# A fp32 network kernel: one 512-column product takes the place of two 256-column ones, and a preparation is spread over two stages

## The chip, the core and the metric

The kernel runs on one core of a Trainium2 chip. The metric is device time in microseconds (us) of one execution. Three runs of the kernel before gave 1077.32 us as the median (1076.91 to 1077.44).

## What is computed

Two layers on 256 tokens (S = 256) of width 1024 (D), in float32. Each layer is a SwiGLU of half weight, a mixer, a second SwiGLU of half weight and a gated embedding ("ple"), each behind an RMS norm. The mixer of layer 0 ("even") holds latent attention and gated linear attention, that of layer 1 ("odd") a gated linear recurrence (RG-LRU) and a complex diagonal state space (S5). What matters here:

```python
def rms_norm(x, g):
    y = x * lax.rsqrt(jnp.mean(x * x, axis=-1, keepdims=True) + EPS)
    return y * g

def swiglu(x, w1, w3, w2):          # D -> 2816 -> D
    return (jax.nn.silu(x @ w1) * (x @ w3)) @ w2

def even_mixer(xn, w_in, ...):
    c_q, c_kv, k_r, gq, gk, gv, g_low, g_r = split_cols(xn @ w_in, EVEN_IN_SPLITS)
    y_a = mla(c_q, c_kv, k_r, ...)
    y_b = gla(gq, gk, gv, g_low, g_r, ...)
    return jnp.concatenate([y_a, y_b], axis=-1) @ w_out

def odd_mixer(xn, w_in, ...):
    x_gate, x_rg, u = split_cols(xn @ w_in, ODD_IN_SPLITS)
    y_c = rg_lru_branch(x_gate, x_rg, ...)
    y_d = s5_branch(u, ...)         # a_re, a_im, log_dt, b, c: parameters only
    return jnp.concatenate([y_c, y_d], axis=-1) @ w_out
```

## The kernel before

**Layout.** Activations lie transposed: 128 channels on the partitions, 256 tokens in the free dimension, so the state h is eight tiles of 128x256. TensorE (PE) multiplies a 128x128 block of weights, which it holds, by a "moving" operand of 256 columns. Float32 accuracy comes from splitting both operands into a high part, a cast to the type fp32r, and a low part, the rest. A step of 128 inner channels (a **k-step**) is three products into the same half bank of PSUM (`mm3`, L260 to L266): high weights by high x (L264), high weights by low x (L265), low weights by high x (L266). Each product is preceded by a load of its weights (PEld).

**Weights** come once from memory. `fetch` (L230 on) issues a transfer of a 128x1024 chunk (SyncE, L242) into one of five raw buffers, ScalarE (ACT) casts the high part wh (L244), VectorE (DVE) subtracts to give the low part wl (L245); five pairs are in flight. A chunk serves one **group** of eight k-steps.

**Norms.** x = h times a gain is split at once (`feed`, ACT L307 and DVE L308); the squares are summed over channels (`stat` L312 on, L351), the reciprocal root R is made by a chain of small operations on GpSimd (POOL, L327 to L340), spread to all partitions by two PE transposes (L365) and a copy on ACT (L367). R is multiplied in only behind the first product, so PE starts a stage without it. `first4` (L272 on) runs the first four groups with the k-steps outermost, since x arrives tile by tile.

**Stages.** The order is ffn_a0, mix0, ffn_b0, ple0, ffn_a1, mix1, ffn_b1, ple1. In a SwiGLU (`ffn`, L377 on) **w1** is 44 groups (22 values of f, two groups each, 352 k-steps): the two groups of one f fill the halves of one PSUM bank, and the epilogue makes ab = bank times R (DVE, L388, 128x512), silu (ACT), s = their product (DVE, L393), and its split into gh (ACT, L289) and gl (DVE, L290). In **w2** (176 k-steps) each of eight output tiles m takes 22 k-steps over gh and gl, and h is updated by one DVE operation (L439). PSUM has five banks "mm" and three "aux". The first stage has its own hand-written start of three f, with squares on POOL.

**What sets the order.** In the mixers and at the start the order on PE is written by hand; everywhere else a scheduler orders each engine's queue when the kernel is built. A queue runs strictly in that order. The even mixer begins with `first4` and two more groups, whose six results are scaled by R into the latents cc (DVE L614, L627) and split after a gain (DVE L625), with squares added (L621); then PE goes to `linear_q`, two groups with the weights gq0 and gq1. The odd mixer begins with `first4` for the S5 input: four results times R, written in another order of tokens (us, DVE L1173), moved in blocks to other partitions (u4, copies on DVE L1178 and ACT), and multiplied into states (PE L1136), which a recurrence on DVE turns into XS (L1139 to L1155); outputs are PE L1163. ple0 scales its gate products by R (DVE, z, L470).

**S5 preparation** (`s5_prep`, L902 on) depends on parameters only: many operations of 128x16 and some of 128x256 on DVE. It is cut into steps, which `beside` puts between the groups of ffn_a1, two for every f up to 16 and three for every m from 1 on. Two of its results lie in x buffer A.

## Time and profile before

| | us |
|---|---|
| median of three runs | 1077.32 |
| span of the profiled execution, first to last instruction | 1074.8 |
| TensorE busy | 1047.1 |
| VectorE busy | 755.6 |
| ScalarE busy | 567.5 |
| GpSimd busy | 83.8 |

The span is 2.5 us shorter than the median; what lies outside of it is the launch. A matmul's start is measured, its end is modelled, and matmuls overlap in the rows, so the cost of one is read as the distance from its start to the next one's start, not as the duration in its row. A row with "x3" holds three instructions in one stretch. Where the clock of TensorE was at its lower level (1.2 GHz), "PEclk" in a table of stretches is 0.50; at 2.4 GHz it is 1.00.

### The profile page before, as it was taken

The numbers are of one execution on the slowest core, as the hardware profiler recorded it, in microseconds if no ns is written. First come the engines' busy times: TensorE is split into PE (matmuls) and PEld (weight loads), VectorE is DVE, ScalarE is ACT, GpSimd is POOL, SyncE is SP. The second block draws the span as 40 slices with busy tenths as digits, with TensorE's granted clock in tenths as the row PEclk, the third lists the DMA queues.
The fourth block names the chain that finished last, engine by engine and source line by source line (L and its number), as shares of the span: only waits on it lengthen the run. The fifth ranks groups of instructions, "written<-read, shape, count | busy, mean of one in ns | idle before, by whom it ended". The sixth has DMA issues, their size and how long they took to land.

```text
span 1074.8 us, 21027 instructions
## 1 busy us (share of the span) xinstructions
PE 1047.1 (97%) x8540; PEld 1025.4 (95%) x8540; DVE 755.6 (70%) x1298; ACT 567.5 (53%) x891; POOL 83.8 (8%) x180
## 2 busy tenths in 40 slices
PE   8899999989999999999999999999998999999996
PEld 7899999979799999999999999999897999999996
DVE  6766665487576766656589986877977766666664
ACT  5444444356465544445555664643778554444553
POOL 6200000230000000000151000002100000000000
PEclk8999999998999999999999999999999999999999
DMA  7655556554235655566626655555223555555651
GB/s 238 214 179 182 181 181 198 169 184 134 85 100 156 235 183 189 168 187 197 216 88 208 196 196 186 182 183 176 74 94 133 182 182 187 181 178 183 189 178 40
DMA packets 52690, 182.56 MB, mean 170 GB/s; under 512 B 5856, under 2 KB 6256, under 8 KB 52592
## 3 DMA queue, kind: packets, MB, share of 16 engines
q1 hardware_dynamic: 52592, 181.20, 52.1%
q8 instruction: 67, 1.10, 0.4%
q14 instruction: 31, 0.25, 0.1%
HBM read 180.13 MB, written 1.05 MB: 169 GB/s over the span
## 4 chain that ended last, share of the span: by engine, by line
PE 91%; DVE 3%; ACT 3%; POOL 2%; issue 1%; DMA 1%; SPq 0%; ACTq 0%; DVEq 0%; POOLq 0%
PE mm L264 27%; PE mm L266 27%; PE mm L265 27%; DVE wl L245 1%; PE aux L1121 1%; PE aux L1136 1%; ACT us L1166 1%; PE mm L501 1%; PE mm L503 1%; PE mm L502 1%; PE mm L715 1%; PE mm L717 1%; DMA h<-in_xT_dram 1%; PE mm L716 1%; PE mm L807 0%
## 5 line engine op out<-in xcount | busy, mean ns | idle before, releaser
L245 DVE TENSOR_TENSOR wl<-raw,wh 128x1024 fp32r<-128x1024 f32 (+2 forms) x350 | 420.9, 1207 | 159.1 <-ACT wh L244 158.1
L244 ACT CAST wh<-raw 128x1024 fp32r<-128x1024 f32 (+2 forms) x350 | 354.6, 1019 | 280.2 <-PE mm L265 128.6
L265 PE MATMUL mm<-xlA,wh 128*128 128x256 f32 x1200 | 341.8, 285 | 1.6 <-DVE xlA L308 1.6
L264 PE MATMUL mm<-xhA,wh 128*128 128x256 f32 x1200 | 341.4, 285 | 1.7 <-ACT xhA L307 1.7
L266 PE MATMUL mm<-xhA,wl 128*128 128x256 f32 x1200 | 340.6, 284 | 0.1
L265 PEld LDWEIGHTS mm<-xlA,wh 128*128 128x128 f32 x1200 | 231.2, 193 | 2.8 <-DVE xlA L308 2.7
L264 PEld LDWEIGHTS mm<-xhA,wh 128*128 128x128 f32 x1200 | 231.5, 193 | 1.9 <-ACT xhA L307 1.9
L266 PEld LDWEIGHTS mm<-xhA,wl 128*128 128x128 f32 x1200 | 231.5, 193 | 0.3 <-DVE wl L245 0.3
L264 PE MATMUL mm<-gh,wh 128*128 128x256 f32 x704 | 195.0, 277 | 0.0
L265 PE MATMUL mm<-gl,wh 128*128 128x256 f32 x704 | 194.9, 277 | 0.0
L266 PE MATMUL mm<-gh,wl 128*128 128x256 f32 x704 | 194.8, 277 | 0.0
L264 PE MATMUL mm<-xhB,wh 128*128 128x256 f32 x576 | 165.1, 287 | 2.5 <-DVE z L470 2.5
L266 PE MATMUL mm<-xhB,wl 128*128 128x256 f32 x576 | 164.1, 285 | 0.0
L265 PE MATMUL mm<-xlB,wh 128*128 128x256 f32 x576 | 164.1, 285 | 0.0
L266 PEld LDWEIGHTS mm<-gh,wl 128*128 128x128 f32 x704 | 132.2, 188 | 0.0
L264 PEld LDWEIGHTS mm<-gh,wh 128*128 128x128 f32 x704 | 132.2, 188 | 0.0
L265 PEld LDWEIGHTS mm<-gl,wh 128*128 128x128 f32 x704 | 132.0, 188 | 0.0
L264 PEld LDWEIGHTS mm<-xhB,wh 128*128 128x128 f32 x576 | 111.8, 194 | 2.7 <-issue 2.6
L265 PEld LDWEIGHTS mm<-xlB,wh 128*128 128x128 f32 x576 | 111.7, 194 | 0.0
L266 PEld LDWEIGHTS mm<-xhB,wl 128*128 128x128 f32 x576 | 111.6, 194 | 0.0
L289 ACT CAST gh<-s 128x256 fp32r<-128x256 f32 x88 | 35.5, 406 | 90.0 <-DVE s L393 90.0
L388 DVE TENSOR_TENSOR ab<-mm,R 128x512 f32<-128x512 f32 x82 | 56.4, 689 | 34.1 <-PE mm L266 31.9
(404 smaller groups left out, 1086.1 us busy)
## 6 DMA issues: line engine op xcount, KB each, us to landing
raw<-in_w_dram SPq DMA_DIRECT2D x308, 512.0 KB, 3.7
raw<-in_w_dram SPq DMA_DIRECT2D x36, 384.0 KB, 3.1
raw<-in_w_dram SPq DMA_DIRECT2D x6, 256.0 KB, 4.2
h<-in_xT_dram SPq DMA_DIRECT2D x4, 256.0 KB, 5.6
out_dram<-hg SPq DMA_DIRECT2D x4, 256.0 KB, 2.2
bd<-in_bd_dram SPq DMA_DIRECT2D x1, 512.0 KB, 4.6
gain<-in_fnorm_dram SPq DMA_DIRECT2D x1, 512.0 KB, 4.2
...
```

Source lines behind the costliest of these rows:

```text
L244: nc.scalar.copy(wh[:, sl], raw[:, sl])
L245: self.last_split = nc.vector.tensor_sub(wl[:, sl], raw[:, sl], wh[:, sl].bitcast(F32))
L264: mm(out, wh, xh, start=start, stop=False)
L265: mm(out, wh, xl, start=False, stop=False)
L266: mm(out, wl, xh, start=False, stop=stop)
L289: self.nc.scalar.copy(hi, src)
L388: nc.vector.tensor_mul(ab, src[0].rearrange("p (t s) -> p t s", t=2), R[:, None, :].to_broadcast([P, 2, S]))
L501: mm(pt, a, wh, start=k == 0, stop=False)
L502: mm(pt, b, wh, start=False, stop=False)
L503: mm(pt, a, wl, start=False, stop=k == KD - 1)
L715: mm(pg[name][i], a, wh, start=k == 0, stop=False)
L716: mm(pg[name][i], b, wh, start=False, stop=False)
```

## The change

**Products.** The tiles of x and of the SwiGLU's inner result become one tile each, in which the high and low part of a k-tile lie side by side ([P, KD, 2, S], [P, NF, 2, S]). `mm2` takes the place of `mm3` where these move past weights: one product of 512 columns (high weights by high and low part) into a whole bank of PSUM, and one of 256 columns (low weights by high part) into its lower half. A k-step is two products and two weight loads instead of three. The halves of the bank are added afterwards: `joined` copies the upper half to SBUF on ACT (128x256) and adds the lower on DVE (128x256); in w2 and in the mixers' output product, h is updated twice instead. `mm2` is used in all of w1 (1408 k-steps) and w2 (704), the input of the even mixer (48), the S5 input and the recurrence's two inputs in the odd mixer (96), both mixers' output products (128) and ple0's gate (64), 2448 k-steps in all. The linear attention's q and k, the latent up-projections, the token-major products and the last embedding keep three products. A SwiGLU's f takes two banks instead of one.

**Preparation.** `s5_prep` starts in ffn_b0 and stops at a mark behind the output matrices; the rest runs in ffn_a1, its input matrices last. `beside` is called once for every f and three times for every m. The tiles that the preparation keeps are allocated before ffn_b0 instead of before ffn_a1, so the SwiGLU's inner tile g lies at another address in ffn_b0 too.

In the built program PE has 5725 rows in its order instead of 8189 (repeats in one row), DVE 1485 instead of 1262, ACT 1021 instead of 820.

```diff
...
+    def mm2(self, out, w, c, x2, start, stop):
+
+        mm = self.nc.tensor.matmul
+        wh, wl = w[0][:, c : c + P], w[1][:, c : c + P]
+        both = x2.rearrange("p t s -> p (t s)")
+        if stop and not start:
+            mm(out[:, :S], wl, x2[:, 0, :], start=False, stop=False)
+            mm(out, wh, both, start=False, stop=True)
+        else:
+            mm(out, wh, both, start=start, stop=False)
+            mm(out[:, :S], wl, x2[:, 0, :], start=False, stop=stop)
+
+    def proj2(self, out, w, c0, x, nk):
+        for k in range(nk):
+            self.mm2(out, w, c0 + k * P, x[:, k], k == 0, k == nk - 1)
+
+    def joined(self, dst, pt):
+
+        self.nc.scalar.copy(dst, pt[:, S:])
+        self.nc.vector.tensor_add(dst, pt[:, :S], dst)
+        return dst
...
-        pts = [self.psum()[:, :S] for _ in range(4)]
+        pts = [self.psum() for _ in range(4)]
...
-                self.mm3(pts[j], ws[j], k * P, P, x[0][:, k, :], x[1][:, k, :], k == 0, k == KD - 1)
+                self.mm2(pts[j], ws[j], k * P, x[:, k], k == 0, k == KD - 1)
...
-        return [self.t(self.xp, [P, KD, S], f"x{part}{buf}", F32R) for part in "hl"]
+        return self.t(self.xp, [P, KD, 2, S], f"x{buf}", F32R)
...
-            gh, gl = (self.t(gp, [P, NF, S], n, F32R) for n in ("gh", "gl"))
-
-            def epilogue(f, src):
-                ab = self.t(gp, [P, 2, S], "ab", bufs=3)
-                s = self.t(gp, [P, S], "s", bufs=3)
-                if len(src) == 1:
-                    nc.vector.tensor_mul(ab, src[0].rearrange("p (t s) -> p t s", t=2), R[:, None, :].to_broadcast([P, 2, S]))
-                else:
-                    for t in range(2):
-                        nc.vector.tensor_mul(ab[:, t, :], src[t], R)
-                nc.scalar.activation(s, ab[:, 0, :], AF.Silu)
+            g = self.t(gp, [P, NF, 2, S], "g", F32R)
+
+            def pair():
+                return self.t(gp, [P, 2, S], "ab", bufs=3)
+
+            def epilogue(f, ab):
+                s = ab[:, 0, :]
+                nc.vector.tensor_mul(ab, ab, R[:, None, :].to_broadcast([P, 2, S]))
+                nc.scalar.activation(s, s, AF.Silu)
                 nc.vector.tensor_mul(s, s, ab[:, 1, :])
-                self.split(gh[:, f, :], gl[:, f, :], s)
...
             for f in range(first, NF):
-                pt = self.psum()
+                ab = pair()
                 for t in range(2):
-                    self.proj(pt[:, t * S : (t + 1) * S], self.weights(), 0, x, KD)
-                    if f < F_SIDE:
-                        self.beside(side)
-                epilogue(f, [pt])
+                    pt = self.psum()
+                    self.proj2(pt, self.weights(), 0, x, KD)
+                    self.joined(ab[:, t, :], pt)
+                epilogue(f, ab)
+                self.beside(side)
...
-                pt = self.psum()[:, :S]
+                pt = self.psum()
                 for a, b in W2_PARTS:
                     w = self.weights()
                     for f in range(a, b):
-                        self.mm3(pt, w, (f - a) * P, P, gh[:, f, :], gl[:, f, :], f == 0, f == NF - 1)
-                    if m >= M_SIDE:
-                        self.beside(side)
+                        self.mm2(pt, w, (f - a) * P, g[:, f], f == 0, f == NF - 1)
+                    self.beside(side)
                 hm = self.h[:, m, :]
-                nc.vector.scalar_tensor_tensor(out=hm, in0=pt, scalar=0.5, in1=hm, op0=ALU.mult, op1=ALU.add)
+                for part in (pt[:, S:], pt[:, :S]):
+                    nc.vector.scalar_tensor_tensor(out=hm, in0=part, scalar=0.5, in1=hm, op0=ALU.mult, op1=ALU.add)
...
+            cc = self.t(self.xp, [P, 6, S], "xB")
+            mg = T([P, S], "mg")
             for j in range(2):
-                self.proj(pm[:, j * S : (j + 1) * S], self.weights(), 0, x, KD)
-            cc = self.t(self.xp, [P, 5, S], "xhB")
-            ch, cl = T([P, 5, S], "ch", F32R), T([P, 5, S], "cl", F32R)
+                pts.append(self.psum())
+                self.proj2(pts[-1], self.weights(), 0, x, KD)
+                if j == 0:
+                    for m in range(2):
+                        self.joined(cc[:, m, :], pts[m])
...
+                if m >= 2:
+                    self.joined(cc[:, m, :], pts[m])
+                nc.vector.tensor_mul(cc[:, m, :], cc[:, m, :], R)
...
-                V.tensor_mul(us[:, t].rearrange("p j m -> p m j"), pts[t].rearrange("p (m j) -> p m j", j=L4), R.rearrange("p (m j) -> p m j", j=L4))
+                z = self.joined(self.t(self.tp, [P, S], "z", bufs=3), pts[t])
+                V.tensor_mul(us[:, t].rearrange("p j m -> p m j"), z.rearrange("p (m j) -> p m j", j=L4), R.rearrange("p (m j) -> p m j", j=L4))
...
+        yield "half"
...
-                if nxt == "mix1":
+                if st == "ffn_b0":
                     s5 = ctx.enter_context(self.tc.tile_pool(name="s5", bufs=1))
                     prep = self.s5_prep(s5, "A")
-                self.ffn(nxt, "B" if nxt == "mix1" else "A", prep, n > 0 and STAGES[n - 1][:3] == "ple")
+                self.ffn(nxt, "B" if nxt == "mix1" else "A", half(prep) if st == "ffn_b0" else prep, n > 0 and STAGES[n - 1][:3] == "ple")
...
```

`half` passes the steps of its argument on up to the mark.

**DVE at the front of the even mixer**, where the latents are made and the weights of `linear_q` are split (its two low parts are wl_417 and wl_420 before, wl_412 and wl_415 after; xhB or xB holds the latents cc, mm_360 and mm_363 the last group's result). Before:

```order
L614 TENSOR_TENSOR xhB_367_2660<-mm_353_2477,R_359_2585 128x256
L621 TENSOR_TENSOR rb_374_2678<-ra_372_2671,sq_373_2676 128x256
L245 TENSOR_TENSOR wl_417_2736<-raw_415_2734,wh_416_2735 128x1024
L245 TENSOR_TENSOR wl_420_2766<-raw_418_2764,wh_419_2765 128x1024
L625 SCALAR_TENSOR_TENSOR cl_369_2662<-xhB_367_2660,cst_1_73,ch_368_2661 128x256
L614 TENSOR_TENSOR xhB_367_2660<-mm_360_2599,R_359_2585 128x256
L627 TENSOR_TENSOR mg_378_2694<-mm_360_2599,R_359_2585 128x256
L245 TENSOR_TENSOR wl_426_2819<-raw_424_2817,wh_425_2818 128x1024
L621 TENSOR_TENSOR kr_377_2690<-sq_375_2683,sq_376_2688 128x256
L625 SCALAR_TENSOR_TENSOR cl_369_2662<-xhB_367_2660,cst_1_73,ch_368_2661 128x256
L245 TENSOR_TENSOR wl_429_2837<-raw_427_2835,wh_428_2836 128x1024
L245 TENSOR_TENSOR wl_433_2862<-raw_431_2860,wh_432_2861 128x768
```

After:

```order
L653 TENSOR_TENSOR rb_372_2202<-ra_370_2193,sq_371_2200 128x256
L657 SCALAR_TENSOR_TENSOR ch_367_2184<-xB_357_2132,cst_1_73,ch_367_2184 128x256
L646 TENSOR_TENSOR xB_357_2132<-xB_357_2132,R_356_2122 128x256
L657 SCALAR_TENSOR_TENSOR ch_367_2184<-xB_357_2132,cst_1_73,ch_367_2184 128x256
L290 TENSOR_TENSOR mg_358_2133<-mm_363_2161,mg_358_2133 128x256
L653 TENSOR_TENSOR kr_375_2218<-sq_373_2209,sq_374_2216 128x256
L657 SCALAR_TENSOR_TENSOR ch_367_2184<-xB_357_2132,cst_1_73,ch_367_2184 128x256
L659 TENSOR_TENSOR mg_358_2133<-mg_358_2133,R_356_2122 128x256
L244 TENSOR_TENSOR wl_412_2263<-raw_410_2261,wh_411_2262 128x1024
L244 TENSOR_TENSOR wl_415_2293<-raw_413_2291,wh_414_2292 128x1024
L244 TENSOR_TENSOR wl_421_2346<-raw_419_2344,wh_420_2345 128x1024
L244 TENSOR_TENSOR wl_424_2364<-raw_422_2362,wh_423_2363 128x1024
```

The two wl operations of `linear_q` moved from among the latents' operations to behind all of them, joins (L290) included.

**DVE in w1 of the second SwiGLU of layer 0 (ffn_b0)**, in the middle of the stage. The L290 rows of before split the inner result, which L311 does after; those of after are joins. Before, five rows are the work of one f:

```order
L245 TENSOR_TENSOR wl_664_4382<-raw_662_4380,wh_663_4381 128x1024
L393 TENSOR_TENSOR s_642_4237<-s_642_4237,ab_641_4236 128x256
L290 TENSOR_TENSOR gl_589_3873<-s_642_4237,gh_588_3872 128x256
L245 TENSOR_TENSOR wl_667_4412<-raw_665_4410,wh_666_4411 128x1024
L388 TENSOR_TENSOR ab_650_4304<-mm_643_4243,R_611_4009 128x512
```

After, with steps of the preparation (128x16):

```order
L244 TENSOR_TENSOR wl_664_3773<-raw_662_3771,wh_663_3772 128x1024
L923 TENSOR_SCALAR esk_632_3618<-esk_632_3618 128x16
L412 TENSOR_TENSOR ab_635_3636<-ab_635_3636 128x256
L924 SCALAR_TENSOR_TENSOR esr_631_3617<-esk_632_3618,esr_631_3617 128x16
L952 TENSOR_SCALAR sk_644_3693<-sk_644_3693 128x16
L290 TENSOR_TENSOR ab_651_3704<-mm_652_3705,ab_651_3704 128x256
L925 SCALAR_TENSOR_TENSOR esr_631_3617<-esk_632_3618,esr_631_3617 128x16
L311 TENSOR_TENSOR g_582_3345<-ab_635_3636,g_582_3345 128x256
L926 TENSOR_SCALAR esp_633_3619<-esr_631_3617 128x16
L930 TENSOR_SCALAR esk_632_3618<-esk_632_3618 128x16
L956 SCALAR_TENSOR_TENSOR sr_645_3694<-sk_644_3693,sr_645_3694 128x16
L928 SCALAR_TENSOR_TENSOR esp_633_3619<-esp_633_3619,esr_631_3617 128x16
```

Two joins for each f and operations of the preparation came between the wl operations.

**DVE at the front of the odd mixer**, from the first result of `first4` to the copies into u4. Before:

```order
L1173 TENSOR_TENSOR us_1347_9270<-mm_1337_9145,R_1346_9256 128x64x4
L1173 TENSOR_TENSOR us_1347_9270<-mm_1338_9146,R_1346_9256 128x64x4
L1173 TENSOR_TENSOR us_1347_9270<-mm_1339_9147,R_1346_9256 128x64x4
L1173 TENSOR_TENSOR us_1347_9270<-mm_1340_9148,R_1346_9256 128x64x4
L245 TENSOR_TENSOR wl_1377_9395<-raw_1375_9393,wh_1376_9394 128x1024
L1178 COPY u4_1348_9275<-us_1347_9270 32x256 x8
L1183 TENSOR_TENSOR xr_1324_9117<-mm_1357_9300,R_1346_9256 128x256
L245 TENSOR_TENSOR wl_1395_9504<-raw_1393_9502,wh_1394_9503 128x1024
L245 TENSOR_TENSOR wl_1405_9593<-raw_1403_9591,wh_1404_9592 128x1024
```

After:

```order
L290 TENSOR_TENSOR z_1333_7783<-mm_1322_7689,z_1333_7783 128x256
L1208 TENSOR_TENSOR us_1332_7782<-z_1333_7783,R_1331_7772 128x64x4
L244 TENSOR_TENSOR wl_1364_7911<-raw_1362_7909,wh_1363_7910 128x1024
L290 TENSOR_TENSOR z_1334_7787<-mm_1323_7690,z_1334_7787 128x256
L290 TENSOR_TENSOR z_1335_7791<-mm_1324_7691,z_1335_7791 128x256
L1208 TENSOR_TENSOR us_1332_7782<-z_1334_7787,R_1331_7772 128x64x4
L1208 TENSOR_TENSOR us_1332_7782<-z_1335_7791,R_1331_7772 128x64x4
L290 TENSOR_TENSOR z_1336_7795<-mm_1325_7692,z_1336_7795 128x256
L290 TENSOR_TENSOR z_1348_7845<-mm_1344_7822,z_1348_7845 128x256
L1208 TENSOR_TENSOR us_1332_7782<-z_1336_7795,R_1331_7772 128x64x4
L1219 TENSOR_TENSOR xr_1308_7660<-z_1348_7845,R_1331_7772 128x256
L1213 COPY u4_1337_7799<-us_1332_7782 32x256 x8
```

Five joins and the scaling of the recurrence's first input (xr) now stand ahead of the copies into u4.

## Rows read from the trace of the kernel before

**Rows 1.** Page: the span, busy time by engine, the lines of the ending chain.
```profile
span 1074.8 us, 21027 instructions
...
PE 1047.1 (97%) x8540; PEld 1025.4 (95%) x8540; DVE 755.6 (70%) x1298; ACT 567.5 (53%) x891; POOL 83.8 (8%) x180
...
PE mm L264 27%; PE mm L266 27%; PE mm L265 27%; DVE wl L245 1%; PE aux L1121 1%; PE aux L1136 1%; ACT us L1166 1%; PE mm L501 1%; PE mm L503 1%; PE mm L502 1%; PE mm L715 1%; PE mm L717 1%; DMA h<-in_xT_dram 1%; PE mm L716 1%; PE mm L807 0%
```

**Rows 2.** Timeline of PE in w1 of ffn_a0: start us, duration us, instruction.
```profile
100.14 0.28 PE L264 MATMUL mm<-xhA,wh 128*128 128x256 f32 x1
...
100.50 0.28 PE L264 MATMUL mm<-xhA,wh 128*128 128x256 f32 x1
```

**Rows 3.** Timeline of PE in w2 of ffn_a0, then of ffn_a1.
```profile
179.76 0.28 PE L264 MATMUL mm<-gh,wh 128*128 128x256 f32 x1
...
180.44 0.28 PE L264 MATMUL mm<-gh,wh 128*128 128x256 f32 x1
...
699.78 0.28 PE L264 MATMUL mm<-gh,wh 128*128 128x256 f32 x1
...
700.49 0.28 PE L264 MATMUL mm<-gh,wh 128*128 128x256 f32 x1
```

**Rows 4.** Timeline of PE in mix0: products of 512 columns, x as the held operand.
```profile
229.48 0.39 PE L715 MATMUL mm<-wh,xhA 128*128 128x512 f32 x1
...
230.16 0.39 PE L715 MATMUL mm<-wh,xhA 128*128 128x512 f32 x1
```

**Rows 5.** Timeline of PE in mix1: twelve products of 64 columns, then the outputs.
```profile
767.75 1.50 PE L1136 MATMUL aux<-u,BT 128*128 128x64 f32 x12
769.09 0.61 PE L1163 MATMUL aux<-XS,cx 128*128 128x64 f32 x4
```

**Rows 6.** Timeline of PE in mix0 at the lower clock.
```profile
244.90 0.41 PE L264 MATMUL mm<-ch,wh 128*128 128x256 f32 x1
...
245.54 0.41 PE L264 MATMUL mm<-xhA,wh 128*128 128x256 f32 x1
```

**Rows 7.** Busy us in stretches: PE, PEld, DVE, ACT, POOL (instructions), PEclk, DMA share, GB/s.
```profile
240.50:247.30 6.80, 6.80 (x29) 6.15 (x30) 1.83 (x3) 4.10 (x5) 0.00 (x0) 0.50 0.24 80
...
600.00:625.00 25.00, 25.00 (x211) 25.00 (x210) 24.65 (x67) 17.53 (x34) 0.00 (x0) 1.00 0.59 198
...
400.00:425.00 25.00, 25.00 (x211) 25.00 (x210) 17.18 (x22) 11.55 (x20) 0.00 (x0) 1.00 0.55 185
```

**Rows 8.** Page, costliest groups: busy us, mean ns of one, idle us before.
```profile
L245 DVE TENSOR_TENSOR wl<-raw,wh 128x1024 fp32r<-128x1024 f32 (+2 forms) x350 | 420.9, 1207 | 159.1 <-ACT wh L244 158.1
...
L388 DVE TENSOR_TENSOR ab<-mm,R 128x512 f32<-128x512 f32 x82 | 56.4, 689 | 34.1 <-PE mm L266 31.9
```

**Rows 9.** Lines by form: duration ns least/median/most, first and last start.
```profile
L391 DVE TENSOR_TENSOR ab<-mm,R x12: 414/416/426, 346.2 to 865.4; 128x256 f32<-128x256 f32 x12
...
L367 ACT COPY R<-aux x7: 367/373/373, 34.5 to 864.0; 128x256 f32<-128x256 f32 x7
```

**Rows 10.** DVE's groups at 600 to 625 us: busy us, mean ns.
```profile
L1074 DVE SCALAR_TENSOR_TENSOR sp<-sp,sp 128x4 f32<-128x4 f32 x8 | 1.3, 157 | 0.1
```

**Rows 11.** Timeline of PE: the transposes of R in ffn_a0 and in mix0.
```profile
34.00 0.43 PE L365 MATMUL aux<-ident,Rt 128*128 128x128 f32 x2 [3.46 <-POOL Rt L340]
...
214.04 0.38 PE L365 MATMUL aux<-ident,Rt 128*128 128x128 f32 x2
```

**Rows 12.** Timeline of POOL in ffn_a0: two steps of the root.
```profile
29.61 1.02 POOL L340 TENSOR_TENSOR Rt<-Rt,rt 128x2 f32<-128x2 f32 x1
30.71 0.20 POOL L334 TENSOR_TENSOR rt<-Rt 128x2 f32<-128x2 f32 x1
```

**Rows 13.** Timeline of DVE: latents and wl in mix0, then XS in mix1.
```profile
214.88 1.09 DVE L614 TENSOR_TENSOR xhB<-mm,R 128x256 f32<-128x256 f32 x3 [6.33 <-ACT R L367]
...
219.24 2.35 DVE L245 TENSOR_TENSOR wl<-raw,wh 128x1024 fp32r<-128x1024 f32 x2
...
768.69 0.41 DVE L1155 TENSOR_TENSOR XS<-ct,ct 128x252 f32<-128x252 f32 x1
```

**Rows 14.** What PE waited for: us in total, times, longest.
```profile
PE mm L264 <- DVE z L470: 2.5, 1, 2.5
```

More of the change, by code (lines that the diff above doesn't have):

```diff
@@ L566, in out_proj @@
         for m in range(KD):
-            w, pt = self.po[m] if m < 4 else (self.weights(), self.psum()[:, :S])
+            w, pt = self.po[m] if m < 4 else (self.weights(), self.psum())
             for n in range(4 if m < 4 else 0, KD):
                 k = ks[n]
-                self.mm3(pt, w, k * P, P, y[0][:, k, :], y[1][:, k, :], n == 0, n == KD - 1)
+                self.mm2(pt, w, k * P, y[:, k], n == 0, n == KD - 1)
             hm = self.h[:, m, :]
-            self.nc.vector.tensor_add(hm, hm, pt)
+            for part in (pt[:, S:], pt[:, :S]):
+                self.nc.vector.tensor_add(hm, hm, part)
             self.h_done(m)
@@ L1008, in put @@
                 nc.scalar.copy(dst[r, :, g], src[r])
-        BB = [self.t(self.xp, [P, NST, L4, 32], f"x{part}{xbuf}") for part in "hl"]
         CX = self.t(pool, [P, 2, NST, L4 + 1, 32], "cx")
-        for a in (*BB, CX):
-            nc.gpsimd.memset(a, 0.0)
-        raw = two("s0")
-        nc.sync.dma_start(raw, ins["sb"])
-        cur = two("s1")
-        yield from cmul(*pair(cur), *pair(raw), b(fr, G), b(fi, G), G)
-        for j in (3, 2, 1, 0):
-            for i in range(2):
-                put(BB[i][:, :, j, :], cur[:, i])
-            if j:
-                prev, cur = cur, two("s" + str((j + 1) % 2))
-                yield from cmul(*pair(cur), *pair(prev), b(are, G), b(aim, G), G)
+        nc.gpsimd.memset(CX, 0.0)
         cur = two("s1")
@@ L1080, in s5_prep @@
         self.decay = cf, e1
+        BB2 = self.t(self.xp, [P, 2, NST, L4, 32], f"x{xbuf}")
+        BB = [BB2[:, i] for i in range(2)]
+        nc.gpsimd.memset(BB2, 0.0)
+        raw = two("s0")
+        nc.sync.dma_start(raw, ins["sb"])
+        cur = two("s1")
+        yield from cmul(*pair(cur), *pair(raw), b(fr, G), b(fi, G), G)
+        for j in (3, 2, 1, 0):
+            for i in range(2):
+                put(BB[i][:, :, j, :], cur[:, i])
+            if j:
+                prev, cur = cur, two("s" + str((j + 1) % 2))
+                yield from cmul(*pair(cur), *pair(prev), b(are, G), b(aim, G), G)
+        self.s5 = BB, CX, rot, m4
     def mix_odd(self, nxt, buf):
@@ L1342, in run, with half @@
                 ctx.close()
+def half(steps):
+    for mark in steps:
+        if mark:
+            return
+        yield
 def flat2(a):
```

92 lines of the change are left out of this document (48 added, 44 removed).

## The prediction

> **What bounds the kernel now.** I read the page's head first: TensorE is busy for 1047.1 us of a span of 1074.8, VectorE for 755.6, ScalarE for 567.5, and the three lines of `mm3` make 81% of the chain that ended last [rows 1]. So time is won only where PE's products get shorter, and lost where PE begins to wait. Then I read, in the timeline, how far the starts of products lie apart. In w1 two starts of L264 lie 0.36 us apart, three products of 0.120 [rows 2]. In w2 two k-steps of ffn_a0 take 0.68 us, so 0.340 each or 0.113 a product; two of ffn_a1 take 0.71, so 0.355 [rows 3]. Three products of 512 columns take 0.68, so 0.227 each [rows 4]: twice 0.113, not twice 0.120. Products of 64 columns come every 1.34/12 = 0.112 us [rows 5], a quarter of the columns in the time of 256: what they wait for can only be the load of their 128x128 weights. So a product of 256 columns stands just where its weight load and its columns cost alike, and the extra 0.007 in w1 looks like a load that takes 0.120 there. A product of 512 columns hides any such load.
>
> **Products, part by part.** A k-step becomes one product of 512 columns and one of 256. No row shows that pair. The 512 costs 0.2267 by its nearest rows [rows 4]; the 256 in w1 costs 0.1200 [rows 2]. Together 0.3467 for 0.3600: 13.3 ns saved. The bounds: if the extra vanishes in both, 0.3400 (20 ns saved); if it also lies on each 512, 0.3533 (6.7 ns saved); if it grows with the columns, 0.3600 (nothing saved). I take 0.3467, because the 512 rows come from the same x and the same weight buffers and show no extra. In w2 the pair costs 0.2267 + 0.1133 = 0.3400, as before.
> - w1 of ffn_a0 behind its start: 304 k-steps x 13.3 ns = -4.05 us. Its first 48 k-steps end before R does: PE waits 3.46 us for the root [rows 11], whose POOL steps take 1.02 us while VectorE splits weights and 0.20 when it doesn't [rows 12]. Their 0.64 us only lengthens that wait, unless the root too moves; I take -0.4, between -1.4 and +0.5.
> - w1 of the three other SwiGLUs: 1056 x 13.3 ns = -14.1 us.
> - w2: 0 in ffn_a0 and ffn_b1. The inner tile g now lies in ffn_b0 where the rows of ffn_a1 had it, behind the S5 tiles. There I price 0.2267 + 0.120: +1.2 us in ffn_b0 (176 x 6.7 ns) and -1.5 in ffn_a1 (from 0.355). Together -0.3.
> - Mixers' inputs and outputs, 48 + 96 + 128 = 272 k-steps x 13.3 ns = -3.6 us.
> - ple0: 64 k-steps, but PE waits there 2.5 us for VectorE's z [rows 14], and z now needs a join. I take 0, between -0.85 and +0.5.
>
> **Joins.** A join is an ACT copy of 0.37 us and a VectorE add of a 128x256 PSUM operand, 0.42 by L391 [rows 9]. One f in w1 costs VectorE now 2 x 1.207 + 0.689 + 2 x 0.42 = 3.9 us [rows 8, 9]; 17.18 us in 25 [rows 7] are 3.96 in the 5.76 us of an f. With two joins it is 4.8, against 16 x 0.3467 = 5.55 us on PE: hidden, with 0.75 us to spare. A join for group n stands ahead of the wl of group n + 4, so PE has about 11 us in hand. The second update of h (0.42 each) runs beside the next tile's products. Cover gone, each join would cost 0.42 on the path.
>
> **S5 preparation.** In ffn_b0 up to about 13 operations of 128x16 fall on one f, at 0.157 [rows 10] 2.0 us, which makes 6.8 us against 5.55. That holds for four or five f, so VectorE falls back by some 6 us, less than the 11 in hand, and catches up later. Before, VectorE had 24.65 us of 25 busy with the same work beside PE at 25.00 [rows 7]. I take 0 and keep up to +6 in the range.
>
> **A new wait in the even mixer.** At 214.04 PE makes R's transposes [rows 11]; 0.84 us later VectorE starts on the latents [rows 13]. Before, the two low parts for `linear_q` came among these operations, from 219.24 to 221.6 [rows 13], the first a microsecond before PE, with 20 k-steps of 0.360 to go, came to them at 221.5. After, wl_412 stands behind all of them. Counted from the transposes, PE is through with its 20 remaining k-steps at 0.3 + 20 x 0.3467 = 7.2 us. VectorE has 0.84 + about 20 operations of 128x256 at 0.36 (their distance in the first row of [rows 13], 1.09/3) to 0.42, and two wl at 1.2: 10.4 to 11.6 us. PE stalls 3.2 to 4.4 us; I take +4.0, as the joins also wait for ACT. Behind wl_412 queue wl_415 and the token-major weights, each needed later than it comes.
>
> **A new wait in the odd mixer.** XS was done at 769.10 just as PE began L1163 at 769.09 [rows 5, 13]: no slack. Five joins and xr, six operations of 0.42 or 2.5 us, now stand ahead of u4; one can run before R is there. I take +2.1, between 0 and 2.5.
>
> **Clock.** After waits the granted clock fell to half for stretches like 240.5 to 247.3, 6.8 us [rows 7], half of which is lost. Whether the new waits bring one more I can't tell: 0 to +3.4, I take +1.0.
>
> **Sum** against the profiled span: -0.4 - 4.05 - 14.1 - 0.3 - 3.6 + 4.0 + 2.1 + 1.0 = -15.35, so 1074.8 becomes 1059.5. The median is 2.5 above the span: **1062 us**.
>
> **Rivals.**
> - *The extra lies on every product* (k-step 0.3533). For it: it is constant in w1 and comes with an address in w2, as if it were tied to reading x. Against it: 512-column products show none. Halving w1's and the mixers' gains gives -9.1 - 1.8; w2 +2.35 - 0.3; waits 7.1, start -0.4: -2.2, **1075**.
> - *The extra was the load alone and vanishes* (0.3400). For it: with a third fewer loads nothing may be late. Against: the load behind a 256 has no more cover than before. w1 -27.2, mixers -5.4, w2 -2.6, waits 7.1, start -0.4: -28.5, **1049**.
> - *Slower: time goes with columns.* Per k-step 768 columns pass before and after. For it: at the lower clock three products take 0.64 us, 0.213 each [rows 6], which is 256 columns at 1.2 GHz and nothing else; and 512 cost twice 0.113. Then the extra of w1 grows too, a k-step stays at 0.360, ffn_b0's w2 loses 2.6 us and the waits 7.1: about +9.7, **1087**. It decides from a k-step of 0.355 on, where 1632 x 5 ns pay for the waits.
> - *VectorE behind in ffn_b0 or ffn_a1* by up to the 6 us above, on top of the forecast: 1068. For it: both stages are the fullest for VectorE. Against it: the 11 us that PE has in hand; it decides only where the arrears pass them.
>
> The rule that speaks most against the change is in the Trainium skill, "TensorE: Matmul & The Clock Gate", section "Back-to-back issue gap": an isolated warm product takes its columns at 2.4 GHz plus 2.5 ns. By it a k-step saves one fixed cost, 2.5 ns, so 2448 k-steps save 6 us, and the waits of 7.1 make it 1078. The trace does not agree with its size: it gives 109 and 216 ns for 256 and 512 columns where the rows have 113 to 120 and 227 [rows 2 to 4]. It counts as a form of the third rival.
>
> **Chances.** Forecast 0.50, extra on every product 0.18, extra gone 0.14, columns 0.12, VectorE behind 0.06. A measurement tells about 0.2% (2.15 us) from no change. Forecast, extra gone and VectorE behind are faster (0.70); the second case, at the very border, I split, 0.08 faster and 0.08 same, with 0.02 slower; the third is slower, but for 0.01 in "same". That makes faster 0.78, same 0.09, slower 0.13. The range 1048 to 1077 takes in the cases at 1049, 1062, 1068 and 1075 and leaves out the one at 1087 and the tails of the outer two, some 0.16 together.
>
> **What would show it.** In the timeline of w1, starts of the 512 product 0.347 us apart, 0.227 and 0.120 within; 0.340, 0.353 or 0.360 name the rival. In w2 0.340. VectorE below 25 in 25 us nearly everywhere, and no PE wait on wl in w1. One PE wait of some 4 us for wl at the first product of `linear_q` and one or two for XS in mix1. The prediction is wrong if the pair costs more than the sum of its rows, if PE waits for a free bank (two per f now, of five), or if VectorE's queue makes PE wait in ffn_b0.

## The result: slower, and the profile after

The changed kernel takes 1083.46 us (median of five runs, 1081.59 to 1087.27) beside 1077.44 us for the kernel before in the same comparison: a ratio of 1.0055, 95% interval 1.0036 to 1.0073. The forecast was 1062 us, with 1048 to 1077 as its range. The profiled execution after has a span of 1081.8 us, 7.0 more than before.

The head of its page:

```profile
span 1081.8 us, 16602 instructions
...
PE 1046.5 (97%) x6092; PEld 909.5 (84%) x6092; DVE 830.3 (77%) x1542; ACT 626.3 (58%) x1092; POOL 84.0 (8%) x179
...
```

PE has 2448 products fewer and is busy for the same time as in [rows 1]: 1046.5 us for 1047.1. Weight loads fell from 95% to 84% of the span, and PE's busy time did not follow them. VectorE rose by 75 us, ScalarE by 59; that alone costs nothing.

**The price of the pair.** L278 is the 512-column product of the last k-step of a group. From its first to its last start in a stretch a k-step's mean follows. Line of L278 in w1 of ffn_a0, then in w2 of ffn_a0, ffn_b0 and ffn_a1 (count, duration ns least/median/most, first to last start):

```profile
L278 PE MATMUL mm<-xA,wh x28: 396/398/400, 61.9 to 138.1; 128*128 128x512 f32 x28
...
L278 PE MATMUL mm<-g,wh x7: 394/394/394, 156.4 to 203.0; 128*128 128x512 f32 x7
...
L278 PE MATMUL mm<-g,wh x6: 397/398/398, 484.6 to 523.2; 128*128 128x512 f32 x6
...
L278 PE MATMUL mm<-g,wh x7: 397/397/398, 697.9 to 744.3; 128*128 128x512 f32 x7
```

w1: 76.2 us over 27 x 8 k-steps, 0.3528 us where [rows 2] had 0.360. w2: 46.6/132 = 0.3530 in ffn_a0 where [rows 3] had 0.340, 38.6/110 = 0.3509 in ffn_b0, 46.4/132 = 0.3515 in ffn_a1. The pair costs 0.351 to 0.353 wherever it stands. The timeline of PE in w1:

```profile
100.22 0.40 PE L280 MATMUL mm<-xA,wh 128*128 128x512 f32 x1
100.45 0.28 PE L281 MATMUL mm<-xA,wl 128*128 128x256 f32 x1
100.57 0.40 PE L280 MATMUL mm<-xA,wh 128*128 128x512 f32 x1
...
100.93 0.40 PE L280 MATMUL mm<-xA,wh 128*128 128x512 f32 x1
```

The 512 takes 0.23 to 0.24, the 256 0.12; over w1 of ffn_a0 the means are 0.235 and 0.117. So the 512 carries an extra of 8 to 9 ns beyond the 0.2267 of [rows 4], and the 256 is 3 ns cheaper than the 0.120 of before.

**The waits.** What PE waited for, after (us in total, times, longest):

```profile
PE aux L386 <- POOL Rt L361: 5.5, 3, 2.7
PE mm L280 <- DVE z L290: 3.5, 2, 2.6
PE mm L265 <- DVE wl L244: 3.5, 1, 3.5
PE mm L263 <- ACT z L1273: 3.4, 2, 2.8
...
PE aux L1170 <- ACT BT L1148: 1.8, 1, 1.8
```

The third row is the wait foretold for `linear_q`. The second is ple0's, longer than in [rows 14]; the first holds a new 2.0 us between ple0 and ffn_a1, and the last is new in mix1. The clock was at half for longer as well: first stretches in ffn_a0, ple0, the front of ffn_a1 and mix1 after (columns as in [rows 7], PEclk third from the end), then stretches in the start, ple0 and mix1 before. At the start it was the kernel before that had the lower clock:

```profile
32.00:40.00 8.00, 7.86 (x37) 6.78 (x38) 4.86 (x9) 4.08 (x9) 0.08 (x1) 0.79 0.61 211
...
552.00:560.00 8.00, 6.35 (x22) 5.53 (x23) 6.86 (x18) 4.28 (x11) 1.37 (x2) 0.57 0.20 67
568.00:572.00 4.00, 3.89 (x17) 3.37 (x18) 2.78 (x10) 3.40 (x6) 3.51 (x2) 0.69 0.40 131
...
832.00:836.00 4.00, 4.00 (x16) 3.52 (x15) 3.52 (x7) 2.78 (x5) 0.00 (x0) 0.53 0.59 160
```

```profile
8.00:12.00 4.00, 2.98 (x12) 2.33 (x11) 4.00 (x5) 3.53 (x8) 3.84 (x6) 0.55 1.04 405
...
548.00:556.00 8.00, 6.29 (x40) 6.32 (x41) 7.97 (x29) 3.28 (x9) 0.61 (x1) 0.79 0.49 166
...
824.00:828.00 4.00, 4.00 (x23) 4.00 (x22) 3.75 (x5) 3.84 (x7) 0.00 (x0) 0.57 0.35 102
```

**Where the 7.0 us came from.** The transposes of R mark the stages. Two of them in ple0 and ffn_a1, before and then after:

```profile
533.41 0.43 PE L365 MATMUL aux<-ident,Rt 128*128 128x128 f32 x2 [0.71 <-POOL Rt L340]
...
562.11 0.38 PE L365 MATMUL aux<-ident,Rt 128*128 128x128 f32 x2
```

```profile
534.78 0.43 PE L386 MATMUL aux<-ident,Rt 128*128 128x128 f32 x2 [0.87 <-POOL Rt L361]
...
568.11 0.43 PE L386 MATMUL aux<-ident,Rt 128*128 128x128 f32 x2 [1.98 <-POOL Rt L361]
```

From one to the next, all seven. The last column is half the length of the stretches at the lower clock, which is the most that they can have cost, in the two executions:

| from R's transposes in | before, us | after, us | change | by the products' prices above | lower clock, us before / after |
|---|---|---|---|---|---|
| (start) | 34.00 | 32.14 | -1.9 | | 3.4 / 0 |
| ffn_a0 | 180.04 | 181.44 | +1.4 | -2.2 + 2.3 | 0 / 1.7 |
| mix0 | 131.32 | 133.74 | +2.4 | -0.8 | 5.1 / 5.1 |
| ffn_b0 | 188.05 | 187.46 | -0.6 | -2.5 + 1.9 | 0 / 0 |
| ple0 | 28.70 | 33.33 | +4.6 | | 1.7 / 3.4 |
| ffn_a1 | 188.10 | 186.55 | -1.6 | -2.5 - 0.3 | 0 / 1.7 |
| mix1 | 113.36 | 115.82 | +2.5 | -1.2 | 1.7 / 3.4 |
| ffn_b1 and ple1 | 211.27 | 211.28 | 0.0 | -2.5 + 2.3 | 0 / 0 up to the last product |

In the SwiGLUs the products' prices and the lower clock explain the stages to within 0.5 us. What w1 won, w2 gave back. The loss lies in mix0, ple0 and mix1, and in the clock. mix0's +2.4 has no clock in it. ple0's +4.6 is 1.0 us more waiting for z, 2.0 for R and 1.7 at the lower clock. Of mix1's +2.5, 1.7 is the lower clock; the other 0.8 is about what the new waits for BT and z (1.8 and 0.9, with 0.5 for BT gone) leave after the products' -1.2. Behind the start the lower clock cost up to 15.4 us where it had cost 8.5.

### The profile page after: what moved, and what is told of

It is laid out like the page before. It is cut to its first block, busy times and chain, and to the rows that moved or that the text cites. A ratio compares the mean times of both kernels' runs of the same rounds, so it can differ in the third digit from the quotient of the medians.

```text
span 1081.8 us, 16602 instructions
## 1 busy us (share of the span) xinstructions
PE 1046.5 (97%) x6092; PEld 909.5 (84%) x6092; DVE 830.3 (77%) x1542; ACT 626.3 (58%) x1092; POOL 84.0 (8%) x179
## 4 chain that ended last, share of the span: by engine, by line
PE 88%; ACT 4%; DVE 3%; POOL 2%; issue 1%; DMA 1%; SPq 0%; DVEq 0%; ACTq 0%; POOLq 0%
PE mm L280 45%; PE mm L281 23%; PE mm L278 5%; PE mm L277 2%; PE mm L263 1%; PE mm L265 1%; PE mm L264 1%; ACT wh L243 1%; DVE wl L244 1%; PE aux L1170 1%; PE mm L527 1%; PE aux L1155 1%; PE mm L529 1%; PE mm L528 1%; PE mm L747 1%
## 5 line engine op out<-in xcount | busy, mean ns | idle before, releaser
L280 PE MATMUL mm<-xA,wh 128*128 128x512 f32 x1022 | 369.3, 401 | 2.7 <-DVE xA L329 2.7
L281 PE MATMUL mm<-xA,wl 128*128 128x256 f32 x1022 | 288.0, 282 | 0.4 <-DVE wl L244 0.4
L280 PE MATMUL mm<-g,wh 128*128 128x512 f32 x672 | 238.1, 396 | 0.0
L280 PEld LDWEIGHTS mm<-xA,wh 128*128 128x128 f32 x1022 | 193.4, 189 | 44.8 <-DVE xA L329 5.0
L281 PEld LDWEIGHTS mm<-xA,wl 128*128 128x128 f32 x1022 | 194.4, 190 | 7.1 <-DVE wl L244 1.2
L280 PE MATMUL mm<-xB,wh 128*128 128x512 f32 x504 | 186.1, 407 | 3.5 <-DVE z L290 3.5
L281 PE MATMUL mm<-g,wl 128*128 128x256 f32 x672 | 188.9, 281 | 0.0
L280 PEld LDWEIGHTS mm<-g,wh 128*128 128x128 f32 x672 | 126.3, 188 | 29.0
L281 PE MATMUL mm<-xB,wl 128*128 128x256 f32 x504 | 143.5, 285 | 0.0
L281 PEld LDWEIGHTS mm<-g,wl 128*128 128x128 f32 x672 | 126.1, 188 | 1.5
L290 DVE TENSOR_TENSOR ab<-mm,ab 128x256 f32<-128x256 f32 x176 | 74.0, 422 | 33.7 <-ACT ab L289 32.8
L278 PE MATMUL mm<-xA,wh 128*128 128x512 f32 x146 | 57.8, 399 | 0.0
L277 PE MATMUL mm<-xA,wl 128*128 128x256 f32 x146 | 41.6, 285 | 0.0
L311 DVE TENSOR_TENSOR g<-ab,g 128x256 fp32r<-128x256 f32 x88 | 36.7, 418 | 4.9 <-ACT g L310 4.9
```

Source lines behind the costliest of these rows:

```text
L277: mm(out[:, :S], wl, x2[:, 0, :], start=False, stop=False)
L278: mm(out, wh, both, start=False, stop=True)
L280: mm(out, wh, both, start=start, stop=False)
L281: mm(out[:, :S], wl, x2[:, 0, :], start=False, stop=stop)
L290: self.nc.vector.tensor_add(dst, pt[:, :S], dst)
L311: self.nc.vector.tensor_sub(lo, src, hi.bitcast(F32))
```

## The experiments

All kernels go back to one of two: the kernel before ("narrow", three products of 256) or the changed one ("wide"). Distances are between the moving and the held operand's byte addresses in a partition, modulo 512; they are the programs' addresses.

**The distance, in narrow.** The rows of before held a hint that the prediction passed over: x with 0.120 lies a multiple of 512 bytes from its weights, the inner tile g with 0.113 lies 192 from them, in ffn_a1 64. One edit moves x to 192:

```diff
-        self.xp = pool("x", 1)
         self.tp = pool("tmp", 2)
+        self.xp = pool("x", 1)
```

> The kernel before, with one edit: the small temporaries are allocated ahead of the x buffers, so that x lies 9408 bytes further from the weights in each partition (192 bytes modulo 512, as the SwiGLU's inner tile does in ffn_a0) instead of a multiple of 512. Theory of addresses (a product's time beyond its columns depends on the distance between moving and held operand): w1 of all SwiGLUs falls from 0.360 to 0.340 us per k-step, w2 stays, the whole falls by about 1700 x 0.020 = 34 us less what waits take, to 1043 to 1050 us. Theory of passes (the extra belongs to the kind of stage or to the pass): 0.360 stays, 1077 us.

Measured: 1051.82 us, ratio 0.977 (0.9748 to 0.9792), a little above the 1043 to 1050 of the address theory. Line of L264 in w1 of ffn_a0, before and then moved; then the moved kernel's ffn_a1:

```profile
L264 PE MATMUL mm<-xhA,wh x223: 283/283/283, 59.8 to 139.7; 128*128 128x256 f32 x112
```

```profile
L264 PE MATMUL mm<-xhA,wh x232: 276/276/276, 60.0 to 138.5; 128*128 128x256 f32 x116
...
L264 PE MATMUL mm<-xhB,wh x213: 281/281/281, 574.7 to 649.7; 128*128 128x256 f32 x107
```

0.3599 us a k-step became 78.5/231 = 0.3398. The same execution shows that it is the distance and not x's own address: ple0's second half takes its weights from another buffer, 320 from x before and 0 after the move. Its k-steps went the other way, from 0.34 to 0.36 (timeline of PE, before and moved):

```profile
541.92 0.28 PE L264 MATMUL mm<-xhA,wh 128*128 128x256 f32 x1
...
542.26 0.28 PE L264 MATMUL mm<-xhA,wh 128*128 128x256 f32 x1
```

```profile
525.99 0.28 PE L264 MATMUL mm<-xhA,wh 128*128 128x256 f32 x1
...
526.35 0.28 PE L264 MATMUL mm<-xhA,wh 128*128 128x256 f32 x1
```

But w1 of ffn_a1 stayed at 75.0/212 = 0.354, and w2 there too.

**The distance, swept in w2.** In the kernel before, a pad ahead of the inner tile:

```diff
+            self.ffns = getattr(self, "ffns", 0) + 1
+            self.t(gp, [P, (80, 32, 48, 64)[self.ffns - 1]], "pad")
             gh, gl = (self.t(gp, [P, NF, S], n, F32R) for n in ("gh", "gl"))
```

> The kernel before with the inner tile g of w2 at 0 (ffn_a0), 320 (ffn_b0), 256 (ffn_a1) and 448 (ffn_b1) bytes modulo 512 from the weights instead of 192, 192, 64 and 192; x stays at 0. Distance theory: w2 of ffn_a0 takes 0.360 us per k-step as w1 does at 0, where it took 0.340; 320 stays at 0.340 (as x in ple0's second half, at 320 from its own weights); the others lie between 0.340 and 0.360. The whole rises by 3.5 us or a little more. Theory that w2 is faster for another reason than distance: 0.340 in all four.

Measured: 1081.51 us (one run), PE at 0.120 with g at 0, as x. Lines of L264 in w2 of ffn_a0 (0), ffn_b0 (320), ffn_a1 (256), ffn_b1 (448):

```profile
L264 PE MATMUL mm<-gh,wh x126: 283/283/284, 159.8 to 204.8; 128*128 128x256 f32 x126
...
L264 PE MATMUL mm<-gh,wh x104: 280/280/281, 489.9 to 526.3; 128*128 128x256 f32 x104
...
L264 PE MATMUL mm<-gh,wh x124: 283/283/284, 700.0 to 744.3; 128*128 128x256 f32 x124
...
L264 PE MATMUL mm<-gh,wh x118: 276/276/277, 999.9 to 1039.7; 128*128 128x256 f32 x118
```

0.360, 0.353, 0.360 and 0.340 (45.0/125, 36.4/103, 44.3/123, 39.8/117). The expectation for 0 held, that for 320 didn't: ple0 had 0.340 there.

**Layout or width.** The kernel before with the interleaved tiles alone:

```diff
-        return [self.t(self.xp, [P, KD, S], f"x{part}{buf}", F32R) for part in "hl"]
+        x = self.t(self.xp, [P, KD, 2, S], f"x{buf}", F32R)
+        return [x[:, :, 0, :], x[:, :, 1, :]]
...
-            gh, gl = (self.t(gp, [P, NF, S], n, F32R) for n in ("gh", "gl"))
+            g = self.t(gp, [P, NF, 2, S], "g", F32R)
+            gh, gl = g[:, :, 0, :], g[:, :, 1, :]
```

> The kernel before with the changed kernel's layout alone: high and low parts interleaved per k-tile in x and in the SwiGLU's inner tile, still three products of 256 columns. If interleaving is what made w2 slower (0.340 to 0.353 us per k-step), w2 shows 0.35 here and the whole 1083 us. If it is the wide product, w2 of ffn_a0 stays at 0.340, w1 at 0.360, and the whole at 1077 us.

Measured: 1075.46 us (one run); w2 of ffn_a0 43.8/129 = 0.340, by its line of L264:

```profile
L264 PE MATMUL mm<-g,wh x130: 276/276/276, 159.8 to 203.6; 128*128 128x256 f32 x130
```

So it is not the layout that made w2 dearer.

**All products wide.** The changed kernel with the low weights' product widened too, so that no widths alternate, with x at 0 and then at 192:

```diff
-        if stop and not start:
-            mm(out[:, :S], wl, x2[:, 0, :], start=False, stop=False)
-            mm(out, wh, both, start=False, stop=True)
-        else:
-            mm(out, wh, both, start=start, stop=False)
-            mm(out[:, :S], wl, x2[:, 0, :], start=False, stop=stop)
+        mm(out, wh, both, start=start, stop=False)
+        mm(out, wl, both, start=False, stop=stop)
```

> The changed kernel with the low weights' product widened to 512 columns as well (it adds low by low, which the reference's accuracy doesn't need). Every product in SwiGLUs has the same width then. Alternation theory: 0.227 each, a k-step of 0.453, the whole near 1083 + 2400 x 0.101 = 1325 us. Theory of an extra on each wide product: 0.235 each, 0.470, the whole near 1365 us.

> The all-wide version with x at 192 bytes from the weights instead of 0. In the all-wide run x at 0 took 0.2267 us a product and g at 192 0.2333. Distance theory, with the sign turned by the width: x now 0.2333 like g, the whole some 1744 x 2 x 0.0066 = 23 us longer, near 1351 us. If x and g differ for another reason, x stays at 0.2267 and the whole at 1328.

Measured: 1328.18 and 1343.46 us (one run each). Lines of L276 (every second product) with x at 0 and g at 192, then x at 192:

```profile
L276 PE MATMUL mm<-xA,wh x221: 389/389/389, 59.9 to 159.7; 128*128 128x512 f32 x111
...
L276 PE MATMUL mm<-g,wh x130: 394/394/394, 194.7 to 254.9; 128*128 128x512 f32 x130
```

```profile
L276 PE MATMUL mm<-xA,wh x215: 398/398/399, 59.9 to 159.7; 128*128 128x512 f32 x108
```

99.8/440 = 0.2268 a product at 0, 60.2/258 = 0.2333 for g at 192, and 99.8/428 = 0.2332 for x at 192. For x the expected prices came in both runs (1351 us was expected of the second, 8 too many); for g the first expectation had 0.227 and 0.235 as its two theories, and 0.2333 lies near the second. At the distance where 256 columns cost most, 512 cost least, and the other way round. The all-wide run also shows the forecast's 0.2267 to be true of x as the moving operand, in that company only.

**The order of the widths.** The changed kernel with runs of one width in a group:

```diff
+        if start:
+            mm(out, part(0, 0), both(0), start=True, stop=False)
+        for k in range(n):
+            mm(out[:, :S], part(k, 1), steps[k][2][:, 0, :], start=False, stop=False)
+        for k in range(1 if start else 0, n):
+            mm(out, part(k, 0), both(k), start=False, stop=stop and k == n - 1)
```

> The changed kernel with the products of a group in another order: one of 512 columns to start, then all of 256 columns (low weights), then the other ones of 512, in w1, in ple0 and mixer groups outside of the four first, and by weight chunk in w2. Theory that the wide pair's extra (0.3525 us for what the rows of before price at 0.340 to 0.347) comes from alternating widths: runs of 512 fall to 0.227 and runs of 256 to 0.113 to 0.120, the k-step to 0.340 to 0.347, the whole by 13 to 25 us to 1058 to 1070. Theory that each product of 512 has its own extra beside x or g as moving operand: 0.235 stays and the whole stays above 1079.

Measured: 1076.13 us (one run), between the two. Lines of L292 (the starting product) in w1 (eight k-steps a group) and w2 (22):

```profile
L292 PE MATMUL mm<-xA,wh x29: 389/389/389, 59.7 to 137.9; 128*128 128x512 f32 x29
...
L292 PE MATMUL mm<-g,wh x6: 393/393/393, 156.1 to 194.4; 128*128 128x512 f32 x6
```

0.3491 and 0.3482 (78.2/224, 38.3/110). So 4 to 5 of the 13 ns beyond 0.340 go with the alternation. The prices of uniform runs by distance, 0.2267 + 0.120 with x at 0 and 0.2333 + 0.1133 with g at 192, make 0.3467 in both; that what is left belongs to the borders between the runs is a guess.

**The distance, in wide.** The changed kernel with x at 192 and g at four other distances (the move of x above, and pads of 80, 48, 80 and 64 words ahead of g):

> The changed kernel with x 192 bytes (modulo 512) from the weights, and the inner tile g of w2 at 0 in ffn_a0, 256 in ffn_b0, 384 in ffn_a1 and 448 in ffn_b1 instead of 192, 64, 64 and 192. Theory of addresses: w1's k-step leaves 0.3525 and w2's differ between the four stages, some at or below 0.340. Theory of passes: w1 stays at 0.352 and w2 at 0.351 to 0.353 everywhere.

Measured: 1084.07 us (one run). Lines of L278 in w1, then w2 of ffn_a0 (0), part of ffn_b0 (256), ffn_a1 (384):

```profile
L278 PE MATMUL mm<-xA,wh x29: 394/394/394, 59.6 to 138.6; 128*128 128x512 f32 x29
...
L278 PE MATMUL mm<-g,wh x7: 395/400/400, 156.9 to 203.4; 128*128 128x512 f32 x7
...
L278 PE MATMUL mm<-g,wh x5: 400/400/400, 492.3 to 523.3; 128*128 128x512 f32 x5
...
L278 PE MATMUL mm<-g,wh x7: 401/401/401, 697.8 to 744.2; 128*128 128x512 f32 x7
```

0.3527, 0.3523, 0.3523, 0.3515: the alternating pair has no good distance among those tried.

**The mixers and ple0.** The changed kernel with three narrow products and no joins there:

```diff
+        if not self.wide:
+            self.mm3(out[:, :S], w, c, P, x2[:, 0, :], x2[:, 1, :], start, stop)
+            return
...
+            self.wide = kind.startswith("ffn")
```

> The changed kernel with three narrow products and no joins in the two mixers and in ple0; the SwiGLUs stay wide. Theory that the joins' place in VectorE's queue makes the new waits of mix0 (3.5 us), ple0 (4.6 us longer stage) and mix1 (2.5 us longer stage): these stages return to 131.3, 28.7 and 113.4 us between R's transposes, and the whole falls by 8 to 9.5 us to about 1075. Rival (the stages are late because the preparation of S5 moved or VectorE arrives with arrears from the SwiGLU before): the stages stay long, the whole stays above 1081.

Measured: 1071.22 us, ratio to before 0.9953 (0.9934 to 0.9971): 12 us better than the whole change, where 8 to 9.5 were expected. A part of it is the clock: the mean granted clock of these executions was 0.984 to 0.994, of the change's 0.977 to 0.985. The two at 0.984 took 1075.3 and 1075.9 us, the change at 0.984 took 1084.0. R's transposes in ple0 and ffn_a1:

```profile
534.05 0.43 PE L391 MATMUL aux<-ident,Rt 128*128 128x128 f32 x2 [0.46 <-POOL Rt L366]
...
561.35 0.38 PE L391 MATMUL aux<-ident,Rt 128*128 128x128 f32 x2
```

ple0 is 27.3 us for 33.3, mix0 131.4 for 133.7, mix1 111.7 for 115.8; 3.4 us each of ple0's and mix1's difference is lower clock that this execution did not have, which leaves 2.6, 2.4 and 0.7 us. PE's 3.5 us for `linear_q`'s wl and 1.8 for BT are gone. So the wide products with their joins cost more in these stages than they save, as the theory of the joins said; that the preparation or arrears made them late is out, since both are still there.

**w2 narrow as well.**

```diff
             self.begin_norm(nxt, buf)
+            self.wide = False
             for m in range(KD):
```

> The SwiGLU-only version (three narrow products in the mixers and ple0) with three narrow products in w2 as well, so that the wide product is left in w1 alone. If w2 lost 0.011 to 0.013 us per k-step to the wide pair, it goes back to 0.340 (0.353 where ffn_a1 had it) and the whole from 1071 to 1065 us. If what w2 lost is the address or the company of the joins, 1071 stays.

Measured: 1069.35 us, ratio to before 0.9935 (0.9909 to 0.996): 1.9 us less than the version above, where 6 were expected. The profiled execution is the fastest of five, with a span of 1064.2 for 1069.6; of these 5.4 us up to 3.4 are lower clock that it did not have. The price is plain all the same. w2 of ffn_a0 is at 42.2/124 = 0.340 again, that of ffn_b0 at 26.5/75 = 0.353:

```profile
L263 PE MATMUL mm<-g,wh x125: 276/276/276, 156.9 to 199.1; 128*128 128x256 f32 x125
...
L263 PE MATMUL mm<-g,wh x76: 279/279/279, 489.8 to 516.3; 128*128 128x256 f32 x76
```

**The preparation alone.** The kernel before with S5's preparation in two SwiGLUs, all products narrow:

```diff
-                if nxt == "mix1":
+                if st == "ffn_b0":
                     s5 = ctx.enter_context(self.tc.tile_pool(name="s5", bufs=1))
...
-                s = self.t(gp, [P, S], "s", bufs=3)
+                s = ab[:, 0, :]
...
```

> The kernel before with the second part of the change alone: the preparation of S5 in ffn_b0 and ffn_a1 (silu in place, to make room), three narrow products everywhere. In the SwiGLU-only version ple0, ffn_a1 and mix1 were shorter than before by 1.4, 2.8 and 1.7 us. If the preparation's move did this, 1072 to 1074 us and these stages shorter here too; if the wide products did, 1077 and no change in mix1 and ple0. Rival: PE waits for VectorE in ffn_b0, above 1078.

Measured: 1081.68 us, ratio 1.0051 (1.0035 to 1.0067): the rival came. ffn_b0 is 192.1 us for 188.05; ple0, ffn_a1 and mix1 are 28.7, 188.1 and 113.4 as before. PE's wait in ffn_b0, and L264 in its w2:

```profile
PE mm L266 <- DVE wl L245: 1.4, 1, 1.4
```

```profile
L264 PE MATMUL mm<-gh,wh x100: 280/280/280, 489.8 to 524.8; 128*128 128x256 f32 x100
```

35.0/99 = 0.3535 a k-step where g now lies at 64, 2.4 us over 176 of them, and 1.4 us of waiting: 3.8 of the 4.0 of the stage. In the changed kernel this wait is absent: in ffn_b0 PE waits for VectorE nowhere. The other stages differ by -1.0 (start), +2.7 (ffn_a0), -1.5 (mix0) and +0.4 (ffn_b1 and ple1); the lower clock does it in ffn_a0 (0.57 from 32 to 40 us, where before had none) and mix0 (3.4 us lost for 5.1).

**A version beyond.** The moved x with two more pads, for ffn_a1's g and for ple0's own weights:

```diff
+            if nxt == "mix1":
+                self.t(gp, [P, 32], "pad")
...
+            self.t(pool, [P, 80], "pad", bufs=1)
```

> The kernel before with x 192 bytes (modulo 512) from the weights as in the first experiment, and two pads: the inner tile g of ffn_a1 at 192 instead of 64, and ple0's own weights moved so that x is at 192 from them as well instead of 0. By the distance theory w2 of ffn_a1 falls from 0.353 to 0.340 us per k-step (-2.3 us) and the second half of ple0 from 0.358 to 0.340 (-0.6 us): 1048 to 1050 us. Whether w1 of ffn_a1, 0.353 in the first experiment after a break in its stream, falls too is open; if it does, another -4.

Measured: 1054.13 us (1049.71 to 1063.13), ratio 0.977 (0.9742 to 0.9798): no better than x alone, and above the 1048 to 1050 expected. The profiled execution is the longest, and shows why it is. Lines of L264 in w1 of ffn_a0 and of ffn_b0, both with x at 192:

```profile
L264 PE MATMUL mm<-xhA,wh x227: 281/281/282, 60.0 to 139.9; 128*128 128x256 f32 x114
...
L264 PE MATMUL mm<-xhA,wh x236: 276/276/277, 370.0 to 449.9; 128*128 128x256 f32 x118
```

79.9/226 = 0.3535 in the one, 79.9/235 = 0.340 in the other, at equal distance. ffn_a1 and ffn_b1 are at 0.3535 too, and so is w2 of all three. Against the first experiment's execution some 1000 k-steps of ffn_a0 and ffn_b1 changed from 0.340 to 0.3535, 13.5 us; the spans differ by 12.4. So at 192 there are two prices, and the pads did not decide which.

## Why the prediction was wrong, point by point

**The pair in w1: mis-sized.** Forecast 0.3467, measured 0.3528. The step that failed is the reason given for the value taken: "the 512 rows come from the same x and the same weight buffers and show no extra". Those rows are products of one width in a row, and in such a row x's 512 do take 0.2267, as the all-wide run shows. Taking turns with 256 they take 0.235, the 256 beside them 0.117. 1360 x 7.2 ns = -9.8 us came, for -18.1 foretold. The first rival's value, 0.3533, is nearly what w1 showed, but not for its reason: x's 512 have no extra of their own at this distance. Of the 13 ns beyond 0.340, sorting the widths removed 4, and 7 are in the uniform prices at the distance; the other 2 stay open.

**The pair in w2: failed.** Taken as 0.3400, "as before", since 0.2267 and 0.1133 have rows. Measured 0.3530, 0.3509, 0.3515: about +6.2 us instead of -0.3. The all-wide runs show why adding rows was no good: a product's price hangs on its distance with a sign that depends on its width, and g's 192, which is the good one for 256, is the bad one for 512. Nothing in before's rows could show that, but the forecast gave w2 no bounds; only the first rival gave it anything, +2.05 us, a third of what came.

**The weight load as the cause of 0.120: not borne out.** 0.120 goes with the distance: g at 0 has it, x at 192 loses it. A product of 512 has a dear distance too, though the prediction had it hide any load. What the operands share no run shows.

**ple0: failed.** Taken as 0, between -0.85 and +0.5; measured +4.6, of which 1.7 is lower clock. The step looked at the groups' savings and not at the chain behind the join: z waits for the bank, the copy on ACT and the add, h and its squares follow, and R of ffn_a1 comes 2 us late. With narrow products there the wait for R was gone and the one for z 2.1.

**mix0: right.** +4.0 foretold, 3.5 measured, at the place and for the wl named; the stage's +2.4 is about that less the products.

**mix1: right in size, wrong in place.** +2.1 foretold for XS; measured was a wait of 1.8 for BT, the next thing on ACT, and 3.4 for the last gate (z L1273), which before's trace has at 2.5, while 0.5 for BT went: +2.2 together. With narrow products there they were gone.

**The start: right in size.** -0.4 taken, -1.4 as the end; -1.9 came, but before's profiled execution had 6.8 us at the lower clock there and after's none. In executions without it the start took 32.9 and 32.8 us with three products (the layout run, the sweep of g) and 32.1 with the pair (the change, the version with w1 alone): -0.7.

**The clock: failed.** +1.0 taken, +3.4 as the most; behind the start it was +6.8, and at the start -3.4. The stretch at the front of ffn_a1 is in the traces of the change, of its sorted version and of its version with x at 192, and in none with narrow products in ple0; the all-wide runs don't have it either. Stretches in other places come and go in kernels whose code there is the same.

**The preparation: right in the change, wrong by itself.** Costed at 0 from VectorE's lead. In the changed kernel ffn_b0 shows no wait for VectorE. Alone it costs 4.0 us there: 1.4 of waiting and 2.4 of g's distance, which the text had priced for the wide product only.

**The sum.** Forecast was -15.35. Measured, by the table: -3.6 from the products of w1 and w2 (-9.8 and +6.2, where the forecast had -18.5), +6.1 in mix0, ple0 and mix1 with their products and without the clock (where it had +2.5), -1.9 at the start (-0.4), +6.8 at most from the lower clock behind it (+1.0): 7.4 for the 7.0 us found. The median lies 1.7 us above the span of the same execution, not 2.5: an execution of the kernel before with a span of 1074.8 took 1076.53. The third rival, that time goes with columns, was nearest with 1087, and by luck: it had 0 from w1, +2.6 from w2 and 7.1 of waits. Three products reach 0.340 at a good distance; no run had two products there, 0.348 with sorted widths being the least.

By the Trainium skill's page "TensorE: Matmul & The Clock Gate", section "Back-to-back issue gap", an isolated product takes its columns at 2.4 GHz plus 2.5 ns, which put the whole at 1078. The runs don't agree with a price by columns alone: 256 columns took 0.1133 to 0.1200 and 512 took 0.2267 to 0.2333, by distance. The page's side of the answer was nearer than the forecast, as the balance of two opposite misses: by the measured prices a k-step won 7.2 ns in w1 and lost 8.8 in w2.

**What is settled by runs and what is not.** That the distance sets the narrow price is shown in both directions within one execution, and w2's loss by w2 made narrow. That the wide products and their joins make mix0, ple0 and mix1 longer is shown for the three together, by their stages and waits; the joins were not tried at another place in the queues. That alternating widths cost 4 to 5 ns a k-step is shown by one run. That the new waits bring the lower clock is not shown. How much of the whole's 6 us each part holds is known only to some 2 us, because stretches at the lower clock come and go between executions of the same code.
